# Two neighbouring K chunks of the split weights interleaved element by element (a step of 8 bytes in the stationary operand)

## The chip, the core and the metric

The kernel runs on one core of one Trainium2 chip. The metric is the device time of one execution in microseconds (us). Work is done by TensorE (PE; its weight loads are listed as PEld), VectorE (DVE), ScalarE (ACT) and GpSimd (POOL); SyncE (SP) only issues transfers.

## The reference

One inference step of a decoder trunk with two layers, for 512 new prompt tokens and 8 x 4 sample tokens that continue stored sequences. Everything is float32, and the model width is 1024.

```python
for i in range(DEPTH):                       # 2
    h = rms_norm(x, norm_mix[i])
    if i % 2 == 0:                           # conformer convolution
        a, gate = jnp.split(h @ w_in + b_in, 2, axis=-1)
        y = causal_dwconv(concat(past, a * sigmoid(gate)), w_dw, b_dw)    # width 31
        out = silu(layer_norm(y, ln_g, ln_b)) @ w_out + b_out
    else:                                    # stick-breaking attention, 16 heads of 64
        q, k, v = split(h @ w_qkv)
        out = stick_breaking(q, concat(cache_k, k), concat(cache_v, v)) @ w_o
    x = x + out
    h = rms_norm(x, norm_ffn[i])
    g = causal_dwconv(concat(past, h @ w_gate), w_dw, b_dw)               # width 3, 2816 channels
    x = x + (silu(g) * (h @ w_up)) @ w_down
y = rms_norm(x, norm_final)
```

Beside `y` for prompt and sample it returns the new convolution states and the new K and V rows. What matters here is the dense products `h @ w`, whose weights are the stationary operand of the matmuls.

## The kernel before

Activations are kept transposed: channels on the 128 partitions, tokens along the free dimension. The 544 tokens go through TensorE in two streams of 256 and 288 columns (SA and SB), or of 272 and 272 in products that join two output columns of `w_gate`, `w_up` or `w_qkv` (slots with sums, below).

**Split operands.** A float32 number is split into two float32r parts, `hi` (the number rounded by a cast) and `lo` (the rest). A dense product takes three matmuls for each K chunk of 128 channels: `hi` of the weights by the high part of the activations, `hi` by the low part, `lo` by the high part. They accumulate in one PSUM tile over all K chunks. In the profile's names `whi` and `wlo` are the weights, and `XH`/`XL`, `HH`/`HL` and `TH`/`TL` are the high and low parts of activations. A matmul of this kind has a weight load (LDWEIGHTS) of 128 columns of its own, with `whi` or `wlo` as the stationary operand.

**The ring of slots.** The class `Ring` (from line 346) brings weights in. `load` fetches a raw tile of up to 8 K chunks by 256 output channels; two raw tiles are in flight. `prep` (line 375) takes one column half of 128 channels and makes a slot of it: two tiles of 128 partitions by 8 chunks by 128 columns, 4 KB a partition each. `high` (line 398) is a cast on ScalarE from the raw tile to `whi`, and `low` (line 401) a subtraction on VectorE, raw minus `whi`, to `wlo`. Most slots are made in one cast and one subtraction of 1024 elements a partition; slots of a `w_down` pass have 4 or 6 chunks (512 or 768 elements), some slots hold sums or differences of two K halves (tile `S`, or raw tiles overwritten in place), and the first slot is made in two halves of 4 chunks. Five slots are kept (`SPLIT_BUFS`), and some stretches have more.

A slot's tile lies chunk after chunk: the 128 columns of chunk k are contiguous, and `hi[:, k, :]` reads 512 bytes of each partition.

**Who reads the slots.** Five places emit the three matmuls for a chunk: `gemm` (lines 495 to 497), `product` of the convolution layer (756 to 758), `part` and `mm` of the feed-forward part (1409 to 1411 and 1630 to 1632), and `weighted` of attention (2126 to 2128). Nothing else reads or writes `whi` and `wlo`.

**The order of work.** `Plan` (class at line 106) holds a list of operations with estimated costs and dependencies, runs them through a small list scheduler and emits the instructions of each engine in the order that comes out. Its costs are numbers in the code and do not depend on how an operand lies in memory.

Other places that the steps of the prediction use: the depthwise convolution as matmuls with 32-column stationary operands (line 893); transposes of the final output (1963); copies of PSUM tiles to SBUF on ScalarE (1668, which writes 8 rows of 4 elements, and 2178); the parameter column copy at line 1078, whose output has a step of 8 elements; the reduction at line 1081, which reads `ident` with a step of 32 elements; and two reductions over contiguous elements (681 and 822).

Of the kernel before, what the change touches and what calls it, by code (L numbers as in the profile page):

```python
# [10 lines left out]
F32R = mybir.dt.float32r  # L11
# [3 lines left out]
ALU = mybir.AluOpType  # L15
PSUM = bass.MemoryType.PSUM

P = 128
D = 1024
NC = D // P  # L20
# [230 lines left out]
def tile_trunk(  # L251
# [9 lines left out]
    dve, act, pool, pe = nc.vector, nc.scalar, nc.gpsimd, nc.tensor  # L261
# [84 lines left out]
    class Ring:  # L346
# [28 lines left out]
        def prep(self, later=None, halves=False):  # L375


            if self.nprep >= len(specs):
                return
            r, kind, last, nk = specs[self.nprep]  # L380
            more = self.more is not None
            home, bufs = (self.more, 1) if more else (ring, SPLIT_BUFS)
            i = self.nprep if more else ""
            hi = home.tile([P, NC, P], F32R, tag=f"whi{i}", name=f"whi{self.nprep}", bufs=bufs)
            lo = home.tile([P, NC, P], F32R, tag=f"wlo{i}", name=f"wlo{self.nprep}", bufs=bufs)
            self.w[self.nprep] = (hi, lo, nk)
            self.nprep += 1
            n = nk
            if kind < 2:
                src = self.raw[r][:, :nk, kind * P:(kind + 1) * P]  # L390
            elif kind == 4:
                n = nk // 2
                src = self.raw[r][:, n:, P:]
            else:
                src = self.sums[r].rearrange("p a k c -> p (a k) c") if kind == 2 else self.raw[r][:, :, 0:P]

            def high(k):
                act.copy(hi[:, k, :], src[:, k])  # L398

            def low(k=slice(0, n)):  # L400
                dve.tensor_tensor(lo[:, k, :], src[:, k], hi[:, k, :], op=ALU.subtract)  # L401
                if last:
                    del self.raw[r]
                    self.load()

            if halves:
                return [lambda f=f, k=k: f(k) for k in (slice(0, n // 2), slice(n // 2, n)) for f in (high, low)]
            high(slice(0, n))
            if later is None:
                low()  # L410
            else:
                later.insert(min(LATER, len(later)), low)
# [2 lines left out]
            self.prep(later)  # L415

    W = Ring()


    ident = base.tile([P, P], F32, name="ident")  # L420
# [9 lines left out]
    XH = base.tile([P, NC, T], F32R, name="XH")  # L430
    XL = base.tile([P, NC, T], F32R, name="XL")
# [57 lines left out]
    def gemm(pt, st, slot, xh, xl, places=None, ks=(0, NF)):  # L489

        hi, lo, nk = W.w[slot]
        c0, n = st
        o = pt[:, :n]
        for k in range(max(0, ks[0]), min(nk, ks[1])):
            pe.matmul(o, hi[:, k, :], xh[:, k, c0:c0 + n], start=(k == 0), stop=False)
            pe.matmul(o, hi[:, k, :], xl[:, k, c0:c0 + n], start=False, stop=False)
            pe.matmul(o, lo[:, k, :], xh[:, k, c0:c0 + n], start=False, stop=(k == nk - 1))
            if places is not None and (k + 1) * 4 // nk > k * 4 // nk:
                for f in places[k * 4 // nk]:
                    f()  # L500
# [16 lines left out]
    def run_group(n, xh, xl, evac, hooked=False, order=(SA, SB), ready=0):  # L517
# [3 lines left out]
        for st in order:  # L521
            last = st is order[-1]
            for i in range(n):
# [6 lines left out]
                if last and hooked:  # L530
                    W.free(side)
                evac(i, st, pt)
                if last and not hooked:
                    W.free()

# [98 lines left out]
    start_cm, start = open_pool("start")  # L634

    xr = [start.tile([P, D], F32, tag=f"xr{b}", name=f"xr{b}") for b in range(4)]
    xs = start.tile([NS, D], F32, name="xs")
# [107 lines left out]
    def product(slot, h):  # L745

        c0, n = STREAMS[h]
        pt = psum("acc")
        last = None
        for q in range(4):  # L750

            def f(q=q):
                hi, lo, _ = W.w[slot]
                o = pt()[:, :n]
                for k in (2 * q, 2 * q + 1):
                    pe.matmul(o, hi[:, k, :], XH[:, k, c0:c0 + n], start=(k == 0), stop=False)  # L756
                    pe.matmul(o, hi[:, k, :], XL[:, k, c0:c0 + n], start=False, stop=False)  # L757
                    pe.matmul(o, lo[:, k, :], XH[:, k, c0:c0 + n], start=False, stop=(k == NC - 1))  # L758

            last = plan.op("pe", 6 * n * 0.46e-3, f, w=[pt], follows=last,  # L760
                    r=[("slot", slot), ("slot", slot, q // 2)] + [(x, k, h) for x in ("XH", "XL") for k in (2 * q, 2 * q + 1)])
        if h:
            ahead = SPLIT_BUFS + (MORE if slot >= 2 * NC else 0)
            if slot + ahead < 2 * NC + NC + SPLIT_BUFS:
                prepare(slot + ahead, lambda low: W.free(low), [("slot", slot)])
        return pt
# [475 lines left out]
    for h, (c0, n) in enumerate(STREAMS):  # L1242
        if h:
            layer_norm(1)
        for g in (0, 4):
            for i in range(4):
                c = g + i
                pt = product(s0 + c, h)
                x = xT[:, c, c0:c0 + n]
# [10 lines left out]
    n = SA[1]  # L1260
# [5 lines left out]
    for c in range(NC):  # L1266
        u = plan.tile("u", NC, lambda: nrm.tile("u", NC))
        e, name, cost = on("pool" if c in POOL_U else "dve", n, 1.05e-3, 2.25e-3)
# [33 lines left out]
    def ffn(l, before, after):  # L1302
# [99 lines left out]
        def part(pt, slot, j, xs, n, start, stop, name, rd):  # L1402

            def f():
                hi, lo, _ = W.w[slot]
                o = pt()[:, :n]
                for k, (xh, xl) in enumerate(xs):
                    kw = dict(skip_group_check=True)
                    pe.matmul(o, hi[:, j + k, :], xh, start=(start and k == 0), stop=False, **kw)  # L1409
                    pe.matmul(o, hi[:, j + k, :], xl, start=False, stop=False, **kw)  # L1410
                    pe.matmul(o, lo[:, j + k, :], xh, start=False, stop=(stop and k == len(xs) - 1), **kw)  # L1411

            return plan.op("pe", len(xs) * 3 * n * 0.4615e-3, f, w=[pt], r=[("slot", slot), *rd], follows=name)

# [194 lines left out]
        def products(slots, tags, put):  # L1609

            s0, s1, s2, s3 = slots
            n = HALF
            a, b, y = (psum(tag) for tag in tags)

            def B(i, h):
                return [(XH[:, 4 * i + k, h * n:(h + 1) * n], XL[:, 4 * i + k, h * n:(h + 1) * n]) for k in range(4)]

            def bk(i, h):
                return [z for j in range(2) for z in bkeys(i, h, j)]

            def Tn(i):
                return [(pools["TH"][:, i, k], pools["TL"][:, i, k]) for k in range(4)]

            def mm(pt, slot, j, xs, start, rd):
                def emit():
                    hi, lo, _ = W.w[slot]
                    o = pt()[:, :n]
                    for k, (xh, xl) in enumerate(xs()):
                        kw = dict(skip_group_check=True)
                        pe.matmul(o, hi[:, j + k, :], xh, start=(start and k == 0), stop=False, **kw)  # L1630
                        pe.matmul(o, hi[:, j + k, :], xl, start=False, stop=False, **kw)  # L1631
                        pe.matmul(o, lo[:, j + k, :], xh, start=False, stop=(k == 3), **kw)  # L1632
                return plan.op("pe", 12 * n * 0.4615e-3, emit, w=[pt], r=[("slot", slot), *rd])

            mm(a, s0, 0, lambda: B(0, 0), True, bk(0, 0))
            put("keep 11", a)
            mm(b, s0, 4, lambda: B(1, 0), True, bk(1, 0))
            used(s0)
            put("11", b)
            mm(y, s1, 0, lambda: Tn(1), True, [("T", 3, 0), ("T", 3, 1)])  # L1640
            mm(a, s2, 0, lambda: Tn(0), False, [("T", 2, 0), ("T", 2, 1)])
            put("keep 21", a)
            mm(a, s1, 4, lambda: Tn(3), False, [("T", 1, 0), ("T", 1, 1)])
            used(s1)
            put("keep 22", a)
            put("22", y)
            mm(a, s2, 4, lambda: B(1, 1), False, bk(1, 1))
            used(s2)
            put("12", a)
            mm(y, s3, 0, lambda: Tn(2), False, [("T", 4, 0), ("T", 4, 1)])  # L1650
            used(s3)
            put("21", y)
# [242 lines left out]
        for p0, pn in rest:  # L1895
# [9 lines left out]
            k0, nk = p0, pn  # L1905
# [141 lines left out]
    for bg in range(2):  # L2047
        for j in range(2):
            rows, src = rows_q(j, bg)
# [68 lines left out]
    def weighted(pt, slot, h, q):  # L2118

        c0, n = (SA, SB)[h]  # L2120

        def f():
            hi, lo, _ = W.w[slot]
            o = pt()[:, :n]
            for k in (2 * q, 2 * q + 1):
                pe.matmul(o, hi[:, k, :], XH[:, k, c0:c0 + n], start=(k == 0), stop=False)  # L2126
                pe.matmul(o, hi[:, k, :], XL[:, k, c0:c0 + n], start=False, stop=False)  # L2127
                pe.matmul(o, lo[:, k, :], XH[:, k, c0:c0 + n], start=False, stop=(k == NC - 1))  # L2128

        return f  # L2130

# [390 lines left out]
    for j in range(2):  # L2522
        rows = slice(j * HD, (j + 1) * HD)
        hi, lo = (X[rows, :, SEQ:T].rearrange("p c (b i) -> p c b i", b=NB) for X in (XH, XL))
# [56 lines left out]
```

## Time and profile before

| | |
|---|---|
| median of 3 runs | 1266.49 us (1265.65 to 1266.7) |
| time of the profiled execution | 1266.66 us |
| span of its trace, first to last instruction | 1265.0 us |
| mean granted TensorE clock | 0.999 |
| busy: PE / PEld / DVE / ACT / POOL | 99 / 95 / 79 / 57 / 13% of the span |
| matmuls | 10,846 records |
| memory traffic | 129.34 MB read, 12.18 MB written |

A row of the profile that lists a group of instructions has the line, the engine, the operation, the tiles as output<-inputs with the numbers of the buffers left out, their shapes (partitions x elements), the count, the busy time in us and the mean of one in ns; behind the next bar stands the idle time of the engine just before them and what ended it. In rows of a matmul or weight load the two tiles are the moving and then the stationary operand. In rows by window the columns are the stretch, its length, and for each engine the busy us with the count of instructions, then the granted clock, the busy share of the DMA engines and GB/s. Matmuls are pipelined, so the busy times of one after another overlap, and the pace is read from their starts.

### The profile page before, as it was taken

How to read it: one execution, taken by the hardware profiler on the slowest of the kernel's cores; microseconds unless marked ns; L12 is line 12 of the kernel's file. 1: busy time of each engine (PE TensorE's matmuls, PEld its weight loads, DVE VectorE, ACT ScalarE, POOL GpSimd, SP SyncE). 2: the span in 40 equal slices, each digit the busy share in tenths (PEclk: the TensorE clock that was granted, in tenths of full speed). 3: DMA queues.
4: the chain of work that ended last, by engine and by line, in shares of the span. 5: the costliest groups of instructions: out<-in, count | busy, mean ns of one | idle time of the engine just before them, and what ended most of it. 6: DMA issues, size and time to landing. Idle time of an engine off the chain costs nothing.

```text
span 1265.0 us, 26475 instructions
## 1 busy us (share of the span) xinstructions
PE 1253.8 (99%) x10846; PEld 1203.5 (95%) x10846; DVE 1004.6 (79%) x1696; ACT 717.2 (57%) x1436; POOL 165.6 (13%) x291
## 2 busy tenths in 40 slices
PE   9999999999999999999999999999999999999998
PEld 8997699999999999999989888999999999999997
DVE  7999886988987887869865589766988987887863
ACT  6794584646645455445565498754645645454453
POOL 5000014111001000002042143200111001000000
PEclk9999999999999999999999999999999999999999
DMA  7465423123233233244355544342223233232221
GB/s 215 127 172 151 128 68 116 34 85 118 92 98 114 67 119 105 71 144 171 117 183 152 157 139 137 114 148 71 65 87 110 84 110 117 67 118 88 89 77 72
DMA packets 119179, 142.39 MB, mean 113 GB/s; under 512 B 5101, under 2 KB 110245, under 8 KB 118786
## 3 DMA queue, kind: packets, MB, share of 16 engines
q1 hardware_dynamic: 110350, 111.89, 28.4%
q0 software_dynamic: 8704, 28.80, 7.2%
q8 instruction: 85, 1.39, 0.5%
q14 instruction: 36, 0.29, 0.1%
q10 hardware_dynamic: 4, 0.01, 0.0%
HBM read 129.34 MB, written 12.18 MB: 112 GB/s over the span
## 4 chain that ended last, share of the span: by engine, by line
PE 84%; DVE 13%; ACT 1%; issue 1%; DMA 0%; DVEq 0%; ACTq 0%
PE acc L1632 5%; PE acc L1631 5%; PE acc L1630 5%; PE acc L756 4%; PE acc L757 4%; PE acc L758 4%; PE av L893 3%; PE av L1409 3%; PE av L1410 3%; PE av L1411 3%; DVE wlo L401 3%; PE tr L1410 3%; PE tr L1409 3%; PE tr L1411 3%; PE tr L1630 3%; PE tr L1632 2%
## 5 line engine op out<-in xcount | busy, mean ns | idle before, releaser
L398 ACT CAST whi<-raw 128x1024 fp32r<-128x1024 f32 (+2 forms) x247 | 224.2, 911 | 119.4 <-PE av L1410 24.9
L401 DVE TENSOR_TENSOR wlo<-raw,whi 128x1024 fp32r<-128x1024 f32 (+2 forms) x247 | 259.2, 1052 | 26.1 <-ACT whi L398 24.8
L756 PE MATMUL acc<-XH,whi 128*128 128x288 f32 (+1 forms) x384 | 112.7, 294 | 0.0
L758 PE MATMUL acc<-XH,wlo 128*128 128x288 f32 (+1 forms) x384 | 110.3, 287 | 0.9 <-DVE wlo L401 0.9
L757 PE MATMUL acc<-XL,whi 128*128 128x288 f32 (+1 forms) x384 | 110.3, 287 | 0.0
L1409 PE MATMUL av<-HH,whi 128*128 128x288 f32 (+1 forms) x280 | 83.2, 297 | 0.4 <-DVE xT L1719 0.4
L1410 PE MATMUL av<-HL,whi 128*128 128x288 f32 (+1 forms) x280 | 82.6, 295 | 0.0
L1632 PE MATMUL acc<-TH,wlo 128*128 128x272 f32 x288 | 82.6, 287 | 0.0
L1631 PE MATMUL acc<-TL,whi 128*128 128x272 f32 x288 | 82.6, 287 | 0.0
L1630 PE MATMUL acc<-TH,whi 128*128 128x272 f32 x288 | 82.6, 287 | 0.0
L2126 PE MATMUL acc<-XH,whi 128*128 128x256 f32 (+1 forms) x264 | 82.0, 310 | 0.6 <-ACT kT L2164 0.6
L1411 PE MATMUL av<-HH,wlo 128*128 128x288 f32 (+1 forms) x280 | 82.2, 294 | 0.0
L1666 ACT COPY G<-acc 128x272 f32<-128x272 f32 (+1 forms) x72 | 26.8, 372 | 93.9 <-PE acc L1632 93.9
L1409 PE MATMUL tr<-HH,whi 128*128 128x256 f32 (+1 forms) x280 | 78.6, 281 | 0.0
L1410 PE MATMUL tr<-HL,whi 128*128 128x256 f32 (+1 forms) x280 | 78.4, 280 | 0.0
L1411 PE MATMUL tr<-HH,wlo 128*128 128x256 f32 (+1 forms) x280 | 78.3, 280 | 0.0
L2128 PE MATMUL acc<-XH,wlo 128*128 128x256 f32 (+1 forms) x264 | 75.8, 287 | 0.0
L2127 PE MATMUL acc<-XL,whi 128*128 128x256 f32 (+1 forms) x264 | 75.7, 287 | 0.0
L756 PEld LDWEIGHTS acc<-XH,whi 128*128 128x128 f32 x384 | 72.2, 188 | 1.4 <-issue 0.4
L758 PEld LDWEIGHTS acc<-XH,wlo 128*128 128x128 f32 x384 | 72.1, 188 | 1.1 <-DVE wlo L401 1.1
L757 PEld LDWEIGHTS acc<-XL,whi 128*128 128x128 f32 x384 | 72.2, 188 | 0.3
L1570 DVE SCALAR_TENSOR_TENSOR cv<-G,fprm,cv 128x560 f32<-128x560 f32 x88 | 69.5, 797 | 0.5
(465 smaller groups left out, 4373.8 us busy)
## 6 DMA issues: line engine op xcount, KB each, us to landing
raw<-in_ffn_w_gate_dram SPq DMA_DIRECT2D x22, 1024.0 KB
raw<-in_ffn_w_up_dram SPq DMA_DIRECT2D x22, 1024.0 KB, 5.4
raw<-in_ffn_w_down_dram SPq DMA_DIRECT2D x24, 768.0 KB, 4.6
raw<-in_attn_w_qkv_dram SPq DMA_DIRECT2D x12, 1024.0 KB, 5.3
raw<-in_conv_w_in_dram POOLq DMA_DIRECT2D x6, 1024.0 KB, 6.9
rep<-glu SPq DMA_DIRECT2D x36, 142.0 KB, 2.9
raw<-in_conv_w_out_dram POOLq DMA_DIRECT2D x4, 1024.0 KB, 6.0
raw<-in_ffn_w_down_dram SPq DMA_DIRECT2D x8, 512.0 KB
```

The lines of the kernel that those rows point to most:

```text
L398: act.copy(hi[:, k, :], src[:, k])
L401: dve.tensor_tensor(lo[:, k, :], src[:, k], hi[:, k, :], op=ALU.subtract)
L756: pe.matmul(o, hi[:, k, :], XH[:, k, c0:c0 + n], start=(k == 0), stop=False)
L757: pe.matmul(o, hi[:, k, :], XL[:, k, c0:c0 + n], start=False, stop=False)
L758: pe.matmul(o, lo[:, k, :], XH[:, k, c0:c0 + n], start=False, stop=(k == NC - 1))
L1409: pe.matmul(o, hi[:, j + k, :], xh, start=(start and k == 0), stop=False, **kw)
L1410: pe.matmul(o, hi[:, j + k, :], xl, start=False, stop=False, **kw)
L1411: pe.matmul(o, lo[:, j + k, :], xh, start=False, stop=(stop and k == len(xs) - 1), **kw)
L1630: pe.matmul(o, hi[:, j + k, :], xh, start=(start and k == 0), stop=False, **kw)
L1631: pe.matmul(o, hi[:, j + k, :], xl, start=False, stop=False, **kw)
L1632: pe.matmul(o, lo[:, j + k, :], xh, start=False, stop=(k == 3), **kw)
L2126: pe.matmul(o, hi[:, k, :], XH[:, k, c0:c0 + n], start=(k == 0), stop=False)
```

## The change

In a slot, chunks 2a and 2a+1 share 256 elements: column c of chunk 2a at place 2c, and column c of chunk 2a+1 at place 2c+1. The tile is allocated as pairs x 128 columns x 2, of the same size as before, and looked at through a rearranged view (pair, chunk in the pair, column). The cast writes `whi` and the subtraction reads `whi` and writes `wlo` with a step of two elements (8 bytes); the raw tile is read as before. The stationary operand of each dense matmul is 128 elements with a step of 8 bytes. All slots are changed and all five readers.

```diff
-            hi = home.tile([P, NC, P], F32R, tag=f"whi{i}", name=f"whi{self.nprep}", bufs=bufs)
-            lo = home.tile([P, NC, P], F32R, tag=f"wlo{i}", name=f"wlo{self.nprep}", bufs=bufs)
+            hi, lo = (home.tile([P, NC // 2, P, 2], F32R, tag=f"w{x}{i}", name=f"w{x}{self.nprep}", bufs=bufs).rearrange(
+                "p a c b -> p a b c") for x in ("hi", "lo"))
...
+            def of(w, k):
+                return w[:, k.start // 2:k.stop // 2]
+
+            def pairs(x):
+                return x.rearrange("p (a b) c -> p a b c", b=2)
+
             def high(k):
-                act.copy(hi[:, k, :], src[:, k])
+                act.copy(of(hi, k), pairs(src[:, k]))
 
             def low(k=slice(0, n)):
-                dve.tensor_tensor(lo[:, k, :], src[:, k], hi[:, k, :], op=ALU.subtract)
+                dve.tensor_tensor(of(lo, k), pairs(src[:, k]), of(hi, k), op=ALU.subtract)
...
+    def chunk_of(w, k):
+        return w[:, k // 2, k % 2, :]
...
-            pe.matmul(o, hi[:, k, :], xh[:, k, c0:c0 + n], start=(k == 0), stop=False)
-            pe.matmul(o, hi[:, k, :], xl[:, k, c0:c0 + n], start=False, stop=False)
-            pe.matmul(o, lo[:, k, :], xh[:, k, c0:c0 + n], start=False, stop=(k == nk - 1))
+            pe.matmul(o, chunk_of(hi, k), xh[:, k, c0:c0 + n], start=(k == 0), stop=False)
+            pe.matmul(o, chunk_of(hi, k), xl[:, k, c0:c0 + n], start=False, stop=False)
+            pe.matmul(o, chunk_of(lo, k), xh[:, k, c0:c0 + n], start=False, stop=(k == nk - 1))
```

The other four readers change in the same way. The instructions of every engine stand in the same order as before and wait for the same; a row of the cast or the subtraction reads 128x4x2x128 where it read 128x1024. From line 381 on a line's number is higher in the changed kernel, by 6 in `prep` and by 9 behind it.

More of the change, by code (lines that the diff above doesn't have):

```diff
@@ L755, in f @@
                 for k in (2 * q, 2 * q + 1):
-                    pe.matmul(o, hi[:, k, :], XH[:, k, c0:c0 + n], start=(k == 0), stop=False)
-                    pe.matmul(o, hi[:, k, :], XL[:, k, c0:c0 + n], start=False, stop=False)
-                    pe.matmul(o, lo[:, k, :], XH[:, k, c0:c0 + n], start=False, stop=(k == NC - 1))
+                    pe.matmul(o, chunk_of(hi, k), XH[:, k, c0:c0 + n], start=(k == 0), stop=False)
+                    pe.matmul(o, chunk_of(hi, k), XL[:, k, c0:c0 + n], start=False, stop=False)
+                    pe.matmul(o, chunk_of(lo, k), XH[:, k, c0:c0 + n], start=False, stop=(k == NC - 1))
             last = plan.op("pe", 6 * n * 0.46e-3, f, w=[pt], follows=last,
@@ L1408, in f @@
                     kw = dict(skip_group_check=True)
-                    pe.matmul(o, hi[:, j + k, :], xh, start=(start and k == 0), stop=False, **kw)
-                    pe.matmul(o, hi[:, j + k, :], xl, start=False, stop=False, **kw)
-                    pe.matmul(o, lo[:, j + k, :], xh, start=False, stop=(stop and k == len(xs) - 1), **kw)
+                    pe.matmul(o, chunk_of(hi, j + k), xh, start=(start and k == 0), stop=False, **kw)
+                    pe.matmul(o, chunk_of(hi, j + k), xl, start=False, stop=False, **kw)
+                    pe.matmul(o, chunk_of(lo, j + k), xh, start=False, stop=(stop and k == len(xs) - 1), **kw)
             return plan.op("pe", len(xs) * 3 * n * 0.4615e-3, f, w=[pt], r=[("slot", slot), *rd], follows=name)
@@ L1629, in emit @@
                         kw = dict(skip_group_check=True)
-                        pe.matmul(o, hi[:, j + k, :], xh, start=(start and k == 0), stop=False, **kw)
-                        pe.matmul(o, hi[:, j + k, :], xl, start=False, stop=False, **kw)
-                        pe.matmul(o, lo[:, j + k, :], xh, start=False, stop=(k == 3), **kw)
+                        pe.matmul(o, chunk_of(hi, j + k), xh, start=(start and k == 0), stop=False, **kw)
+                        pe.matmul(o, chunk_of(hi, j + k), xl, start=False, stop=False, **kw)
+                        pe.matmul(o, chunk_of(lo, j + k), xh, start=False, stop=(k == 3), **kw)
                 return plan.op("pe", 12 * n * 0.4615e-3, emit, w=[pt], r=[("slot", slot), *rd])
@@ L2125, in f @@
             for k in (2 * q, 2 * q + 1):
-                pe.matmul(o, hi[:, k, :], XH[:, k, c0:c0 + n], start=(k == 0), stop=False)
-                pe.matmul(o, hi[:, k, :], XL[:, k, c0:c0 + n], start=False, stop=False)
-                pe.matmul(o, lo[:, k, :], XH[:, k, c0:c0 + n], start=False, stop=(k == NC - 1))
+                pe.matmul(o, chunk_of(hi, k), XH[:, k, c0:c0 + n], start=(k == 0), stop=False)
+                pe.matmul(o, chunk_of(hi, k), XL[:, k, c0:c0 + n], start=False, stop=False)
+                pe.matmul(o, chunk_of(lo, k), XH[:, k, c0:c0 + n], start=False, stop=(k == NC - 1))
         return f
```

## The prediction

> **What bounds the kernel now.** I read the page first (busy time, granted clock, chain), then the tiles of the split weights, then the timeline of TensorE inside two dense stretches, and last the groups by shape.
>
> ```profile
> PE 1253.8 (99%) x10846; PEld 1203.5 (95%) x10846; DVE 1004.6 (79%) x1696; ACT 717.2 (57%) x1436; POOL 165.6 (13%) x291
> ...
> PEclk9999999999999999999999999999999999999999
> ...
> PE 84%; DVE 13%; ACT 1%; issue 1%; DMA 0%; DVEq 0%; ACTq 0%
> PE acc L1632 5%; PE acc L1631 5%; PE acc L1630 5%; PE acc L756 4%; PE acc L757 4%; PE acc L758 4%; PE av L893 3%; PE av L1409 3%; PE av L1410 3%; PE av L1411 3%; DVE wlo L401 3%; PE tr L1410 3%; PE tr L1409 3%; PE tr L1411 3%; PE tr L1630 3%; PE tr L1632 2%
> ```
>
> The kernel is bound by TensorE: 99% of the span, full granted clock, 84% of the chain that ended last. Most of the chain's lines are matmuls on `whi` and `wlo`. VectorE holds 13% of it, and the subtraction that makes `wlo` (L401) about 3%, which is some 38 us. The two tiles alone, over the whole span (whi first, then wlo):
>
> ```profile
> 0.00:1265.00 1265.00, 1085.84 (x5712) 891.78 (x5712) 305.24 (x285) 264.01 (x285) 1.00 0.36 113
> ```
> ```profile
> 0.00:1265.00 1265.00, 820.07 (x2856) 536.92 (x2856) 305.24 (x285) 1.00 0.36 113
> ```
>
> So 5,712 + 2,856 = 8,568 matmuls have a stationary operand that the change touches, each with a weight load of its own. They are made by 285 casts on ScalarE (264.01 us) and 285 subtractions on VectorE (305.24 us). In the program's instruction order 2,688 of the matmuls stream 256 columns, 3,192 stream 272 and 2,688 stream 288. How fast they follow each other is read from the timeline; its columns are start and duration in us:
>
> ```profile
> 701.08 0.28 PE L2128 MATMUL acc<-XH,wlo 128*128 128x256 f32 x1
> 701.08 0.19 PEld L2126 LDWEIGHTS acc<-XH,whi 128*128 128x128 f32 x1
> 701.19 0.28 PE L2126 MATMUL acc<-XH,whi 128*128 128x256 f32 x1
> 701.20 0.19 PEld L2127 LDWEIGHTS acc<-XL,whi 128*128 128x128 f32 x1
> 701.31 0.28 PE L2127 MATMUL acc<-XL,whi 128*128 128x256 f32 x1
> 701.31 0.19 PEld L2128 LDWEIGHTS acc<-XH,wlo 128*128 128x128 f32 x1
> 701.43 0.28 PE L2128 MATMUL acc<-XH,wlo 128*128 128x256 f32 x1
> ...
> 703.52 0.30 PE L2127 MATMUL acc<-XL,whi 128*128 128x288 f32 x1
> 703.66 0.29 PE L2128 MATMUL acc<-XH,wlo 128*128 128x288 f32 x1
> 703.78 0.29 PE L2126 MATMUL acc<-XH,whi 128*128 128x288 f32 x1
> 703.91 0.30 PE L2127 MATMUL acc<-XL,whi 128*128 128x288 f32 x1
> ```
> ```profile
> 401.12 0.29 PE L1630 MATMUL acc<-XH,whi 128*128 128x272 f32 x1
> 401.25 0.28 PE L1631 MATMUL acc<-XL,whi 128*128 128x272 f32 x1
> 401.37 0.29 PE L1632 MATMUL acc<-XH,wlo 128*128 128x272 f32 x1
> ```
>
> From start to start a matmul of 256 columns takes 0.117 us (701.08 to 701.43 in three), one of 288 0.130 (703.52 to 703.91 in three), one of 272 about 0.124. The time grows by 13 ns for 32 columns, so the moving stream sets it. Each load starts together with the matmul before its own, and the next load starts one matmul later: a load has 117 ns at the least before it holds up the stream. The weight loads by shape:
>
> ```profile
> L757 PEld LDWEIGHTS acc<-XL,whi 128*128 128x128 f32 x384 | 72.2, 188 | 0.3
> ...
> L893 PEld LDWEIGHTS av<-rep,wdg 128*32 128x32 f32 x768 | 24.4, 110 | 17.1 <-issue 0.8 <-ACT whi L398 0.3 <-ACT ext_p L898 0.3
> ...
> L1963 PEld LDWEIGHTS yt<-ident,xg 128*128 128x128 f32 x32 | 4.1, 142 | 0.3 <-ACT xg L1948 0.2
> ...
> L1963 PEld LDWEIGHTS yt<-ident,xg 128*32 128x32 f32 x8 | 0.8, 96 | 0.0
> ```
>
> A load of 128 columns takes 188 ns, one of 32 columns 110: 0.81 ns a column, so 104 ns of the 188 go with the columns. The rest is latency, which overlaps, since loads of 188 ns start every 117. The slack of a load is then at most 117 - 104 = 13 ns beside 256 columns, 20 beside 272 and 26 beside 288, and perhaps none, if the gap belongs to the load. This is the number the change plays against.
>
> **The change part by part.** Nothing is moved: on all five engines the instructions stand in the same order, with the same waits, and only the shapes of the cast and the subtraction read otherwise (4 x 2 x 128 for 1024). Slots keep their size, and no DMA changes. Three things are new.
>
> *The weight load.* 128 elements are fetched over 1,024 bytes of a partition where they lay in 512. No stationary operand of the kernel before has a step, so I bound it from both sides. Below: no cost, by the moving operand, which is also read by TensorE and sweeps 256 x 4 = 1,024 bytes in 117 ns (701.08 to 701.19 above), 8.8 bytes a ns; a stepped load needs just that, 1,024 bytes in 117 ns. The load of the transposes (L1963) takes 142 - 96 = 46 ns for 96 columns, 0.48 ns each, so the load side can fetch an element nearly twice as fast as it does for `whi`. Above: twice the bytes take twice the 104 ns. I take no cost, since the row of the moving operand is the same engine at the same sweep. A gain is excluded: the same 8,568 loads remain, and the stream, not the load, sets the pace.
>
> *The cast and the subtraction.* Each of 285 casts writes `whi`, and each of 285 subtractions reads `whi` and writes `wlo`, with a step of 8 bytes. VectorE by shape, then ScalarE:
>
> ```profile
> L401 DVE TENSOR_TENSOR wlo<-raw,whi 128x1024 fp32r<-128x1024 f32 x143 | 175.4, 1228 | 13.0 <-ACT whi L398 12.4
> ...
> L822 DVE TENSOR_REDUCE ext_p<-prod 128x32 f32<-128x992 f32 x8 | 9.5, 1182 | 0.1
> ...
> L1081 DVE TENSOR_REDUCE eye<-ident 128x32 f32<-128x128 f32 x1 | 0.4, 367 | 0.0
> L681 DVE TENSOR_REDUCE bcol<-oh 128x2 f32<-128x32 f32 x1 | 0.2, 185 | 0.0
> ```
> ```profile
> L398 ACT CAST whi<-raw 128x1024 fp32r<-128x1024 f32 x143 | 149.8, 1051 | 61.7 <-PE av L1410 24.5 <-PE acc L757 12.8 <-PE acc L496 5.9
> ...
> L2178 ACT COPY vT<-acc 128x256 f32<-128x256 f32 x16 | 6.0, 376 | 7.2 <-PE acc L2128 7.0
> ...
> L1668 ACT COPY G<-acc 128x32 f32<-128x32 f32 x36 | 7.0, 194 | 0.0
> ...
> L1078 ACT COPY tapc<-av 128x96 f32<-128x96 f32 x2 | 0.6, 384 | 0.0
> ```
>
> Two rows have a real step. L1081 reads `ident` with a step of 128 bytes: the reduces L681 (32 elements, 185 ns) and L822 (992, 1182) give 1.04 ns an element and 152 ns fixed, so 285 ns for 128 elements; it took 367, which is 0.64 ns more for each. L1078 writes with a step of 32 bytes: L1668 (32, 194 ns) and L2178 (256, 376) give 0.81 ns an element and 168 ns fixed, so 246 for 96; it took 384, 1.44 ns more for each. If 8 bytes cost an element as much, a subtraction of 1024 grows by 0.66 us and a cast by 1.47. If the cost goes by bytes swept, those rows went over 128 x 128 bytes in 367 - 152 = 215 ns and over 96 x 32 bytes in 384 - 168 = 216 ns, 76 and 14 bytes a ns; the stepped subtraction needs 8,192 bytes in 1228 - 152 = 1076 ns and the cast 8,192 in 1051 - 168 = 883 ns, 8 and 9 bytes a ns. By that the step is free, and I take free: 8 bytes is the smallest step there is above none, and both instructions go at about an element in 0.9 to 1.1 ns, with no faster mode to lose.
>
> The Trainium skill weighs here too (SBUF — State Buffer, "Door 1: The DMA port swizzle"): SBUF is read in lines of 16 bytes, and two hits on a line are enough for full bandwidth, while an access that goes to a new line each time pays. L1078 and L1081, with a new line for each element, agree that it pays; that two hits are enough no run here shows yet. By the rule the sum is nothing, by the two rows 1.44 and 0.64 ns an element.
>
> *More dimensions.* The out pattern has three free dimensions where there was one. L1668 writes 8 rows of 4 and lies on the line used above, so I price this at nothing.
>
> The sum is 0 us, and what hides it is the slack of the load. The profiled execution took 1266.66 us (span 1265.0 and 1.66 around it), 0.17 over the median of three, 1266.49. I forecast 1266.5.
>
> **The rivals.** *First rival: the load becomes TensorE's bound, at twice its time.* The point from which it decides is 13 ns of lengthening at the most. At 208 ns a load, every matmul is paced by loads: 2,688 x (208 - 117) + 3,192 x (208 - 124) + 2,688 x (208 - 130) ns = 245 + 268 + 210 = +722 us; if the gap of 13 ns comes on top, 8,568 x 13 = 111 us more. That is 1988 to 2100, about 2045 us. For it speaks that no stepped load stands in the trace and that there is hardly any slack; against it the moving operand's sweep. The Trainium skill's sentence on the same page and section, "each access that crosses to a new line pays a penalty", read by itself, would point here, as a stepped load meets 64 lines instead of 32. Chance 0.09.
>
> *Second rival: the load grows a little.* At 10 ns more, if there is no slack beside 256 columns: 2,688 x 10 + 3,192 x 3 ns = 27 + 10 = +36 us, 1303 us; at 2 ns more, 2,688 x 2 = +5 us, 1272. Loads and stream would both be read at about 8.8 bytes a ns, which has no example in the trace. Chance 0.09.
>
> *Third rival: the step costs VectorE and ScalarE per element* as in L1081 and L1078. Two stretches where VectorE is fullest, all of VectorE first, then `wlo` alone:
>
> ```profile
> 50.00:100.00 50.00, 50.00 (x406) 50.00 (x406) 47.48 (x88) 47.52 (x185) 3.53 (x4) 1.00 0.51 149
> ...
> 300.00:350.00 50.00, 49.91 (x401) 49.69 (x401) 47.50 (x73) 30.79 (x52) 4.56 (x12) 1.00 0.33 101
> ```
> ```profile
> 50.00:100.00 50.00, 37.44 (x131) 24.47 (x132) 11.00 (x9) 1.00 0.51 149
> 300.00:350.00 50.00, 38.22 (x134) 25.05 (x133) 19.83 (x18) 1.00 0.33 101
> ```
>
> The subtractions on the chain pay at once: 38 us of them at about 1.2 us are 31, times 0.66 = +20 us. In the two stretches VectorE has 2.5 us left of 50 and gets 9 x 0.66 = 6 and 18 x 0.55 = 10 us more (mixed sizes), so +3.5 and +7.5 us over. Together +31, 1298 us. Elsewhere VectorE (1004.6 us busy) would gain some 161 us and ScalarE (717.2) some 361, both still under the span. Chance 0.12.
>
> *That the change does not do what it says* is no rival: the built program has a step of two elements in every one of these operands.
>
> **How the numbers follow.** No cost 0.68 (own range 1264 to 1269), third rival 0.12, second 0.09, first 0.09, and 0.02 that another placement in memory happens to help. A measurement of this kernel tells about 0.2% from no change, 2.5 us. Faster 0.02, same 0.68, slower 0.12 + 0.09 + 0.09 = 0.30. The range runs from 1264, the lower end of no cost, over the third rival's 1298 to 1300, which takes in most of the second; outside are the first and the top of the second, about 0.1.
>
> **What would show it.** Right: weight loads still at 188 ns, starts 117, 124 and 130 ns apart, casts near 1051 and subtractions near 1228 ns. First and second rival: LDWEIGHTS on `whi` and `wlo` longer, or starts beside 256 columns over 117 ns while those beside 288 move less. Third: L398 and L401 (a few lines further down there) longer at an unchanged load, with TensorE waiting for `wlo`. The forecast is wrong if any of the three durations moves by more than its spread and the time by more than 2.5 us.

## The result

| | before | changed |
|---|---|---|
| median | 1266.6 us (1265.65 to 1267.35, 4 runs) | 1283.23 us (1282.65 to 1283.8, 4 runs) |
| profiled execution, its span | 1266.66, 1265.0 us | 1283.15, 1281.5 us |

The ratio is 1.0132, with a 95% interval of 1.0114 to 1.0149: the changed kernel is slower by 16.6 us. That lies inside the range, but the likeliest case, no cost, did not come.

### The profile page after: what moved, and what is told of

The parts are those of the page before. It is cut to its first block, busy times and chain, and to the rows that moved or that the text cites. A ratio compares the mean times of both kernels' runs of the same rounds, so it can differ in the third digit from the quotient of the medians.

```text
span 1281.5 us, 26475 instructions
## 1 busy us (share of the span) xinstructions
PE 1271.3 (99%) x10846; PEld 1222.9 (95%) x10846; DVE 1005.9 (78%) x1696; ACT 739.2 (58%) x1436; POOL 164.0 (13%) x291
## 5 line engine op out<-in xcount | busy, mean ns | idle before, releaser
L404 ACT CAST whi<-raw 128x1024 fp32r<-128x1024 f32 (+2 forms) x247 | 245.0, 996 | 121.9 <-PE av L1419 26.1
L765 PEld LDWEIGHTS acc<-XH,whi 128*128 128x128 f32 x384 | 75.4, 196 | 1.4 <-issue 0.4
L767 PEld LDWEIGHTS acc<-XH,wlo 128*128 128x128 f32 x384 | 75.5, 197 | 1.1 <-DVE wlo L407 1.1
L766 PEld LDWEIGHTS acc<-XL,whi 128*128 128x128 f32 x384 | 75.6, 197 | 0.3
```

Of the source, the lines that this page charges most:

```text
L404: act.copy(of(hi, k), pairs(src[:, k]))
L765: pe.matmul(o, chunk_of(hi, k), XH[:, k, c0:c0 + n], start=(k == 0), stop=False)
L766: pe.matmul(o, chunk_of(hi, k), XL[:, k, c0:c0 + n], start=False, stop=False)
L767: pe.matmul(o, chunk_of(lo, k), XH[:, k, c0:c0 + n], start=False, stop=(k == NC - 1))
```

## The profile after

The page of the changed kernel, busy time and granted clock:

```profile
PE 1271.3 (99%) x10846; PEld 1222.9 (95%) x10846; DVE 1005.9 (78%) x1696; ACT 739.2 (58%) x1436; POOL 164.0 (13%) x291
...
PEclk9999999999999999999999999999999999999999
```

The same number of instructions runs at the same full clock (mean 0.999 in both). TensorE is busy 17.5 us longer and still 99% of the span. VectorE gained 1.3 us and ScalarE 22.0. Everything that touches the two tiles, `whi` first and then `wlo`:

```profile
0.00:1282.00 1282.00, 1104.39 (x5712) 922.74 (x5712) 305.55 (x285) 288.53 (x285) 1.00 0.36 111
```
```profile
0.00:1282.00 1282.00, 828.65 (x2856) 559.97 (x2856) 305.55 (x285) 1.00 0.36 111
```

The subtractions are where they were (305.55 against 305.24 us), the casts grew by 24.5 us in all, and the busy time of loads and matmuls grew in both tiles. By shape (busy us and mean ns of one behind the first bar):

```profile
L407 DVE TENSOR_TENSOR wlo<-raw,whi 128x1024 fp32r<-128x1024 f32 x143 | 175.6, 1229 | 17.0 <-ACT whi L404 16.6
L404 ACT CAST whi<-raw 128x1024 fp32r<-128x1024 f32 x143 | 164.2, 1152 | 63.6 <-PE av L1419 25.1 <-PE acc L766 12.8 <-PE acc L505 5.8
...
L766 PEld LDWEIGHTS acc<-XL,whi 128*128 128x128 f32 x384 | 75.6, 197 | 0.3
L767 PEld LDWEIGHTS acc<-XH,wlo 128*128 128x128 f32 x384 | 75.5, 197 | 1.1 <-DVE wlo L407 1.1
```

A weight load went from 188 to 197 ns, a cast of 1024 from 1051 to 1152, a subtraction from 1228 to 1229. The rows of cast and subtraction still read 128x1024, not 4 x 2 x 128: a row shows how many elements there are, and not their pattern. TensorE's waits, with the total, the count and the longest, show that nothing comes late: the only wait for `wlo` is as long as before, 0.9 us once. Before, then after:

```profile
PE acc L758 <- DVE wlo L401: 0.9, 1, 0.9
```
```profile
PE acc L767 <- DVE wlo L407: 0.9, 1, 0.9
```

So the time must lie in the pace. Stretches of the timeline with 272, 256 and 288 columns, first and last matmul of each:

```profile
400.01 0.29 PE L1639 MATMUL acc<-TH,whi 128*128 128x272 f32 x1
...
401.93 0.29 PE L1639 MATMUL acc<-TH,whi 128*128 128x272 f32 x1
...
410.27 0.28 PE L1418 MATMUL tr<-HH,whi 128*128 128x256 f32 x1
...
411.47 0.28 PE L1419 MATMUL tr<-HL,whi 128*128 128x256 f32 x1
...
573.50 0.30 PE L1418 MATMUL acc<-HH,whi 128*128 128x288 f32 x1
...
575.77 0.29 PE L1420 MATMUL acc<-HH,wlo 128*128 128x288 f32 x1
```

15 intervals in 1.92 us are 128 ns, 10 in 1.20 us are 120 ns, 17 in 2.27 us are 133.5 ns. Single stretches scatter by a few ns, so I took all pairs of consecutive matmuls on `whi` and `wlo` in each trace, by the width of the first. The mean is over the distances from start to start up to 160 ns, which leaves out 2% of them; the sum is over all pairs, the longer distances included:

| columns | pairs | mean before | mean changed | sum before | sum changed |
|---|---|---|---|---|---|
| 256 | 2,632 | 117.0 ns | 120.2 ns | 317.1 us | 324.9 us |
| 272 | 3,186 | 124.4 | 126.8 | 397.7 | 404.7 |
| 288 | 2,624 | 132.3 | 133.4 | 354.1 | 356.8 |

The sums grow by 7.8 + 7.0 + 2.7 = 17.5 us, against 16.5 us of span. The loss is 1 to 3 ns on average at each of some 8,440 matmuls. The chain that ended last can be followed back only to 825 us in this execution, so its shares are not set beside those of before.

## The experiments

*Theory A* is that the stepped read of the weight load makes it longer, and that the pace suffers. *Theory B* is that the stepped writes of the cast and the subtraction cost the time, through their own length or by disturbing TensorE's reads. The later letters divide theory A further. Where a kernel writes its weights in one layout and loads them in another, a matmul multiplies mixed elements of the same slot; the number and size of its instructions stay.

### The loads alone: stepped reads, contiguous writes

Against the kernel before, one of the five readers and without the branch for left-over chunks:

```diff
-            pe.matmul(o, hi[:, k, :], xh[:, k, c0:c0 + n], ...)
+            pe.matmul(o, chunk_of(hi, k), xh[:, k, c0:c0 + n], ...)
+    def flat(w, k0, nk):
+        return w.t[:, k0:k0 + nk, :].rearrange("p k c -> p (k c)")
+    def chunk_of(w, k):                                   # s = 2
+        return flat(w, k // s * s, s).rearrange("p (c b) -> p c b", b=s)[:, :, k % s]
```

> Cast and subtraction write the slots contiguously as in the kernel before; only the weight loads step by 8 bytes (each chunk of a pair reads every second element of the pair's 256, so the products mix two chunks and the output is not the reference's). Theory A (the stepped load itself takes 8 ns longer and each matmul starts 1 to 3 ns later): about 1283 us, +16 to +17; loads at 196 ns, casts back at 1051 ns, starts 120, 127 and 133 ns apart. Theory B (the stepped writes and reads of ScalarE and VectorE in SBUF slow TensorE's reads): 1266.5 us, loads at 188 ns.

Measured: 1282.88 us (1282.12 to 1283.46), ratio 1.0127 (1.0112 to 1.0143). Loads and casts of this kernel:

```profile
L775 PEld LDWEIGHTS acc<-XL,whi 128*128 128x128 f32 x384 | 75.5, 197 | 0.3
...
L400 ACT CAST whi<-raw 128x1024 fp32r<-128x1024 f32 x143 | 149.8, 1051 | 66.0 <-PE av L1428 25.7 <-PE acc L775 13.7 <-PE acc L514 6.0
```

The load is that of the changed kernel and the cast that of before, and the mean distances are 120.2, 126.8 and 133.4 ns, to the tenth those of the changed kernel. The stepped loads alone give the whole difference.

### The writes alone: stepped casts and subtractions, contiguous reads

Against the changed kernel:

```diff
     def chunk_of(w, k):
-        return w[:, k // 2, k % 2, :]
+        return w.rearrange("p a c b -> p a (c b)")[:, k // 2, k % 2 * P:(k % 2 + 1) * P]
```

> The other half: cast and subtraction step by 8 bytes as in the changed kernel, the weight loads read 128 contiguous elements (half of each of two chunks, so the output is not the reference's). Theory A: 1266.5 us, loads at 188 ns, casts at 1152 ns, subtractions at 1228 ns; the longer casts stay hidden, or cost 1 us at the most. Theory B: about 1283 us with loads at 196 ns.

Measured: 1267.34 us (1266.75 to 1267.94), ratio 1.0005 (0.9996 to 1.0014). The same two groups:

```profile
L404 ACT CAST whi<-raw 128x1024 fp32r<-128x1024 f32 x143 | 163.3, 1146 | 59.6 <-PE av L1419 23.9 <-PE acc L766 11.9 <-PE acc L505 5.7
...
L766 PEld LDWEIGHTS acc<-XL,whi 128*128 128x128 f32 x384 | 72.2, 188 | 0.3
```

The casts are long here and the loads short, and the time is that of before: theory B falls. The casts grow by 23 us in all (264.0 to 287.0), which ScalarE, busy for 57% of the span before, has room for.

### Only `whi` stepped

Against the kernel with the loads alone, one of the five readers:

```diff
-            pe.matmul(o, chunk_of(lo, k), xh[:, k, c0:c0 + n], ...)
+            pe.matmul(o, flat(lo, k, 1), xh[:, k, c0:c0 + n], ...)
```

> As the loads-only kernel, but only the two loads of whi step by 8 bytes, the one of wlo is contiguous; output mixes chunks. Theory A with a cost for each stepped load: two thirds of 16.7, +11, about 1277.6 us, and only the starts that follow a stepped load are later. Rival D (the cost is a slower rhythm of the whole stream, set by the slowest load of the three): over +14 us.

Measured: 1278.32 us (1277.48 to 1278.69), ratio 1.0092 (1.0077 to 1.0108). The loads of both tiles:

```profile
L775 PEld LDWEIGHTS acc<-XL,whi 128*128 128x128 f32 x384 | 74.9, 195 | 0.3
L776 PEld LDWEIGHTS acc<-XH,wlo 128*128 128x128 f32 x384 | 72.7, 189 | 1.1 <-DVE wlo L403 1.1
```

Two thirds of the loads have a step; they cost 1278.32 - 1266.57 = 11.75 us of the 1282.88 - 1266.57 = 16.31 that all of them cost, 0.72. The interval of the ratio, 9.8 to 13.7 us, holds two thirds (10.9) and not the whole: the total goes with the number of stepped loads, and rival D falls. The other half of the expectation, that only the starts that follow a stepped load are later, did not come. Between two matmuls of 256 columns the mean distance grew by 2.7 ns from `whi` to `whi`, by 2.7 from `whi` to `wlo`, where the load that runs meanwhile is contiguous, and by 2.1 from `wlo` to `whi`. Beside 288 columns the same three changed by 0.6, -0.5 and 1.0 ns. So where the slack is used up a delay is not tied to the one load; how it is handed on stays open.

### Steps of 12, 16 and 32 bytes, loads alone

```diff
-        s = 2
+        s = 3        # the second kernel: 4, the third: 8
```

Chunks left over in a slot that s does not divide take the smaller step that fits, a slot with fewer chunks than s takes their number, and the first slot, made in two halves, stays at 4 at most.

> Loads only, with a step of 12 bytes over three chunks (left-over pairs of chunks at 8 bytes), output mixes chunks; 128 elements lie in 96 lines of 16 bytes. Between 8 bytes (196 ns, 120 to 133 ns a start, 1283 us) and 16 bytes (330 ns, 233 ns a start, 2135 us). If the cost goes by lines, 64 lines being nearly free and 128 costing 233 ns, 1.82 ns a line: 96 x 1.82 = 175 ns a start for three quarters of the matmuls, about 1620 us. If only two hits on each line hide the fetch, the single hits cost as in the step of 16 bytes, and the double hits nothing more: about the same 170 to 180. If it jumps to the price of 16 bytes: about 1900 us.

> As the loads-only kernel, but with a step of 16 bytes over four chunks (left-over pairs of chunks in slots of 6 stay at 8 bytes); output mixes chunks. Theory A, cost by new 16-byte lines met (32 contiguous, 64 at 8 bytes, 128 at 16): if each further line costs the 0.26 ns that 8 ns over 32 lines give, the load is 188 + 25 = 213 ns, it binds beside 256 columns, and the time is 1310 to 1350 us; if a second hit on a line is what hides its fetch, the column part of 104 ns doubles, loads are near 290 ns, starts near 220 ns for all widths, and the time is about 2000 to 2100 us. Rival C (any step other than one costs the same): as at 8 bytes, loads 196 ns, 1283 us.

> Loads only, with a step of 32 bytes over eight chunks (24 bytes in slots of 6, 16 in slots of 4 and in the first), output mixes chunks; 128 lines as at 16 bytes, over twice the span. If lines set the cost: as at 16 bytes, 330 ns a load, 233 ns a start, about 2135 us. If the span or a bank pattern counts: longer, over 2200 us.

Measured: 1613.92 us at 12 bytes (1613.32 to 1614.42), ratio 1.2745 (1.2722 to 1.2768); 2135.53 at 16 bytes (2134.8 to 2136.03), ratio 1.6857 (1.6831 to 1.6883); 2233.72 at 32 bytes, one run. The 12 bytes came as expected, where a price by lines and one by single hits give the same; 16 bytes cost more than the dearest case of their expectation (2100 us). The timeline at 12 bytes:

```profile
700.06 0.34 PE L1649 MATMUL tr<-TL,whi 128*128 128x272 f32 x1
...
701.28 0.34 PE L1650 MATMUL tr<-TH,wlo 128*128 128x272 f32 x1
```

and at 16 bytes:

```profile
799.87 0.40 PE L1427 MATMUL av<-HH,whi 128*128 128x288 f32 x1
...
800.57 0.29 PE L1427 MATMUL av<-HH,whi 128*128 128x288 f32 x1
...
801.37 0.39 PE L1427 MATMUL tr<-HH,whi 128*128 128x256 f32 x1
...
802.52 0.40 PE L1429 MATMUL tr<-HH,wlo 128*128 128x256 f32 x1
```

At 12 bytes 7 intervals in 1.22 us are 174 ns beside 272 columns. At 16 bytes 3 intervals in 0.70 us are 233 ns beside 288 columns, and 5 in 1.15 us are 230 beside 256: the width no longer matters, the load sets the pace. Between them stand six matmuls in 0.80 us, 133 ns each. They are a leftover pair of chunks in a slot of six, still read with 8 bytes, so one timeline shows both prices. Over the whole trace a load's own pace is about 175 ns at 12 bytes and 233 at 16. The Trainium skill gives SBUF lines of 16 bytes (SBUF — State Buffer, "Door 1: The DMA port swizzle"). Counted in stretches of 16 bytes, the 128 elements lie on 96 and on 128: 1.82 ns for each, both times. At 8 bytes they lie on 64, which makes 64 x 1.82 = 117 ns.

At 32 bytes each element has a line to itself, as at 16, and twice the bytes are swept, yet the price grows by 3%: it goes by lines far more than by bytes swept. Loads of a full slot and of slots of `w_down`, most of which have six chunks:

```profile
L775 PEld LDWEIGHTS acc<-XL,whi 128*128 128x128 f32 x384 | 130.0, 338 | 0.0
...
L1429 PEld LDWEIGHTS av<-HH,wlo 128*128 128x128 f32 x280 | 90.8, 324 | 0.0
```

The full slots take 338 ns where 16 bytes took 330. The expectation for a price by lines was missed by 98 us, and its limit of 2200 us for another cause was passed, for two reasons of about 48 us each. A further step is not quite free (in the products other than `w_down` the mean distance of starts went from 234 to 241 ns; no run shows why). And the slots of six are now read with 24 bytes in all their chunks, where the kernel with 16 bytes read a third of them as pairs with 8 (there the mean went from 205 to 229).

### The load's own time: short streams behind it

Two of the three matmuls of each chunk stream 64 columns only, so that a load cannot hide; once with contiguous and once with stepped loads (`chunk_of` then returns one chunk as it lies, or every second element). One of the five readers:

```diff
-            pe.matmul(o, chunk_of(hi, k), xl[:, k, c0:c0 + n], ...)
-            pe.matmul(o, chunk_of(lo, k), xh[:, k, c0:c0 + n], ...)
+            pe.matmul(o[:, :64], chunk_of(hi, k), xl[:, k, c0:c0 + 64], ...)
+            pe.matmul(o[:, :64], chunk_of(lo, k), xh[:, k, c0:c0 + 64], ...)
```

> The kernel before with two of the three matmuls of a chunk cut to 64 moving columns (whi by the low part, wlo by the high part; the rest of their columns is left out), so that behind them the stream is over early and the load's own time shows. Its time says nothing; its rows do. Starts from one short matmul to the next should be near the 104 ns that the load's columns were estimated at (100 to 112 ns), loads at 188 ns.

> The same with loads stepped by 8 bytes. Theory A1 (the stepped load is longer by itself): starts behind short matmuls 8 ns later than in the kernel with contiguous loads and short streams, loads at 196 ns everywhere. Theory A2 (the stepped load meets the moving stream at the memory, and both pay): the same starts as with contiguous loads to within 2 ns, loads at 188 to 190 ns where the streams are short. In the dense kernel A1 would need a load of 117 ns or more of its own to move the starts, A2 would not.

Measured: 1804.1 us contiguous and 1887.02 stepped, one run each. These times say nothing of the step, because the granted clock fell, in other places in each run (mean 0.635 and 0.608). The contiguous kernel, its clock and then its timeline at full and at half clock:

```profile
PEclk9999855555555555555559999995555555555555
```
```profile
103.83 0.19 PE L769 MATMUL acc<-XL,whi 128*128 128x64 f32 x1
103.86 0.27 PE L770 MATMUL acc<-XH,wlo 128*128 128x64 f32 x1
103.97 0.38 PE L768 MATMUL acc<-XH,whi 128*128 128x288 f32 x1
...
104.55 0.19 PE L769 MATMUL acc<-XL,whi 128*128 128x64 f32 x1
...
600.42 0.26 PE L1643 MATMUL tr<-TL,whi 128*128 128x64 f32 x1
...
601.07 0.26 PE L1643 MATMUL tr<-TL,whi 128*128 128x64 f32 x1
```

The stepped kernel likewise:

```profile
PEclk6555995555555555555556999999555555555555
```
```profile
262.14 0.20 PE L775 MATMUL acc<-XL,whi 128*128 128x64 f32 x1
262.18 0.28 PE L776 MATMUL acc<-XH,wlo 128*128 128x64 f32 x1
262.29 0.39 PE L774 MATMUL acc<-XH,whi 128*128 128x288 f32 x1
...
264.38 0.20 PE L775 MATMUL acc<-XL,whi 128*128 128x64 f32 x1
...
600.04 0.26 PE L1649 MATMUL acc<-TL,whi 128*128 128x64 f32 x1
...
600.70 0.26 PE L1649 MATMUL acc<-TL,whi 128*128 128x64 f32 x1
```

Compared within stretches of full clock, three matmuls (288, 64 and 64 columns) take 0.72 / 2 = 0.360 us contiguous and 2.24 / 6 = 0.373 stepped; the medians over all such stretches are 356 and 372 ns, twice 8 ns apart. In the interval behind the second short matmul the stream is over early and the load sets the time; at full clock its median is 109 ns contiguous and 117 stepped. So A1 holds: the stepped load itself is 8 ns longer, with no long stream beside it. At half clock three matmuls of 272, 64 and 64 columns take 0.65 and 0.66 us (medians 653 ns in both), and the same interval has a median of 214 ns in both: there the step costs nothing. The contiguous load, 32 lines or 58 ns at 1.82 each, is thus set by something else, which doubles with the half clock (109 to 214 ns); the 117 ns of the stepped one fit under it there.

### Narrower and wider streams

In the convolution layer's products the two column ranges become 224 and 352, once with contiguous and once with stepped loads; the writes are contiguous in both. The ranges overlap, so 32 columns are computed twice, and in the first range the first matmul of a tile keeps its 256 columns. The first of the three matmuls:

```diff
+                    a, m = (c0 - 64, 352) if h else (c0, n if k == 0 else 224)
-                    pe.matmul(o, chunk_of(hi, k), XH[:, k, c0:c0 + n], ...)
+                    pe.matmul(z, chunk_of(hi, k), XH[:, k, a:a + m], ...)
```

> Contiguous loads as in the kernel before, but in the convolution layer's products the matmuls of the first stream have 224 moving columns instead of 256 (the rest is left out) and those of the second 352 instead of 288 (64 columns of the first stream are added in front, so that layer's products are not the reference's). It is the base for the next run. If the load needs 109 ns of its own, it binds at 224 columns (stream 93 ns): starts near 109 to 113 ns; at 352 the stream sets it: 157 to 160 ns. The time itself says little.

> The same widths with all weight loads stepped by 8 bytes. Theory J (a stepped load needs 117 ns, and a matmul pays what its load sticks out over the stream, with some spread): at 224 columns 7 to 9 ns more than with contiguous loads, 117 to 121 ns; at 352 columns no more than 0.5 ns. Theory S (load and stream disturb each other's reads, so every matmul pays something): at 352 columns 1 to 3 ns more as well.

Measured: 1281.3 and 1299.21 us, one run each. The contiguous kernel:

```profile
70.22 0.32 PE L771 MATMUL acc<-XH,whi 128*128 128x352 f32 x1
...
72.94 0.32 PE L773 MATMUL acc<-XH,wlo 128*128 128x352 f32 x1
...
75.11 0.27 PE L771 MATMUL acc<-XH,whi 128*128 128x224 f32 x1
...
76.00 0.28 PE L773 MATMUL acc<-XH,wlo 128*128 128x224 f32 x1
```

The stepped one:

```profile
70.35 0.32 PE L778 MATMUL acc<-XL,whi 128*128 128x352 f32 x1
...
72.94 0.32 PE L779 MATMUL acc<-XH,wlo 128*128 128x352 f32 x1
...
75.13 0.28 PE L777 MATMUL acc<-XH,whi 128*128 128x224 f32 x1
...
76.20 0.28 PE L777 MATMUL acc<-XH,whi 128*128 128x224 f32 x1
```

Beside 352 columns 17 intervals in 2.72 us are 160 ns and 16 in 2.59 us are 162; beside 224, 8 in 0.89 us are 111 and 9 in 1.07 us are 119. The means over the traces, at 224 and 352 columns over pairs of one width with distances up to 200 ns (514 and 547 to 548 pairs in each trace), in the other rows as above:

| columns | contiguous | stepped | more |
|---|---|---|---|
| 224 | 111.5 ns | 118.0 ns | 6.5 |
| 256 | 117.0 | 120.2 | 3.2 |
| 272 | 124.4 | 126.8 | 2.4 |
| 288 | 132.3 | 133.4 | 1.1 |
| 352 | 160.3 | 162.2 | 1.9 |

Beside 224 columns nearly all of the load's 8 ns is paid: the load sets the pace. Were a load that sticks out of its stream the only cost (J), 352 columns, with 160 - 117 = 43 ns to spare, would pay nothing. They pay 1.9, and 288 columns, with 15 to spare, 1.1. So J alone falls; nor does it tell why a contiguous `wlo` load shared the delay when only `whi` was stepped. A second part of 1 to 2 ns a matmul is there beside the two widest streams as well, which S, that load and stream disturb each other, would give. What that part consists of was not settled: no run had a stepped load without a stream to be disturbed and at the same time room to see 1 ns, so S is argued and not shown.

## Why the prediction was partly right and partly wrong

*The range held, in part by luck.* Its upper end came from the third rival, which fell. The case that came, a load that grows a little, had a chance of 0.09.

*The bound was right.* TensorE's pace in the dense stretches sets the time, at full clock, and what moved the time moved that pace and nothing else.

*The length of the load was right, its reason was not.* The prediction gave the stepped load 1,024 bytes in 117 ns, by the sweep of the moving operand. With short streams it takes 117, and at 12 and 16 bytes the sweep gives the measured time too: 1,536 bytes in 175 ns and 2,048 in 233, 8.8 bytes a ns each time. But up to 16 bytes bytes swept and lines met grow together. At 32 bytes they part, and 4,096 bytes took about 241 ns, 17 bytes a ns: the sweep is no bound, while 1.82 ns for each line fits 8, 12 and 16 bytes and is 3% short at 32. That the sweep gave 117 too is luck. The rule of the Trainium skill from the same section, by which two hits on a line are enough for full bandwidth (SBUF — State Buffer, "Door 1: The DMA port swizzle"), agrees nearly: 109 became 117 ns with two hits, and 233 with one.

*The step that failed is "I take no cost, since the row of the moving operand is the same engine at the same sweep".* The load came out as long as its stream of 256 columns, and from that the prediction concluded that it hides. It does not hide for free. The slack was smaller than thought: a contiguous load needs 109 ns, not 104, which leaves 8 beside 256 columns, and the step takes all 8. With none left each matmul pays 3.2 ns. And slack does not protect fully: beside 288 columns the prediction saw 26 ns, the stepped load leaves 15 (132 less 117), and 1.1 ns are paid. Why matmuls with slack pay at all is open, as said above.

*The second rival, a load that grows a little (0.09), is what happened*, with another price. By its sum, without slack beside 256 columns, a growth of 8 ns costs 2,688 x 8 = 22 us there, about 3 beside 272 and nothing beside 288, 25 in all. Measured were 7.8 us, 7.0 and 2.7, 17.5 in all and in other shares. The spread by width went as the prediction asked for in this case: the narrow streams suffer more.

*The first rival* (a load of twice its time, 1988 to 2100 us) needed a step of 16 bytes: there it is the case, 2135.53 us.

*The third rival* fell. The cast pays 101 ns for 1,024 elements, 0.1 ns each, near the free end of the bounds 0 and 1.44, and the subtraction nothing (ends 0 and 0.64). The writes alone moved the time by a ratio of 1.0005 (0.9996 to 1.0014). That a cost by bytes swept leaves the step free agrees with VectorE and fails for ScalarE, where no run shows why. More dimensions cost nothing on VectorE, as priced; on ScalarE no run has the step without them, so its 101 ns belong to the two together.

## What to carry to other kernels

A weight load that hides behind the stream has to be compared with its stream in ns, and a load that is just as long as its stream is not free: here 8 ns on the load cost 1 to 3 ns at each matmul and 1.3% of the time. Keep stationary operands contiguous where matmuls follow one another densely; if a step can't be avoided, 8 bytes cost little, 12 bytes 27% and 16 bytes 69% here. For a loss that is spread over thousands of instructions, take the mean of start-to-start distances by shape: the waits don't show it, and the durations of single loads don't give its size.

## What the runs showed of the hardware

- A weight load of 128 columns of float32 has a pace of its own of 109 ns contiguous, 117 at a step of 8 bytes, 175 at 12, 233 at 16 and about 241 at 32, at full granted clock. At half clock it is 214 ns both contiguous and at 8 bytes.
- With two of three streams cut to 64 columns the granted clock fell to about 0.5 for most of the span, though TensorE's busy share stayed at 99%. What the clock goes by was not tried.
- ScalarE's cast that writes with a step of 8 bytes, in a pattern of 4 x 2 x 128, takes 0.1 ns more an element (1051 to 1152 ns for 1,024), and VectorE's subtraction that reads and writes so nothing (1228 to 1229 ns).
